# One more modulation vector computed in columns, more weight pairs multiplied by seven products, and deeper buffers of the weights' parts

## The chip, the cores and the metric

The kernel runs on one core of one Trainium2 chip. Its time is the device time of one execution in microseconds (us); lower is better. The core has a matrix engine (TensorE, PE in the profile, PEld for its weight loads), a vector engine (VectorE, DVE), an activation engine (ScalarE, ACT), a general engine (GpSimd, POOL), and SyncE (SP), which only issues DMA transfers here. Each engine works its own instructions off strictly in program order and waits on semaphores for the others.

## What is computed

One layer of a conditioned decoder on one sequence of S = 256 tokens with D = 2048 features, all in float32:

```python
mod = silu(c) @ ada_w + ada_b                      # 2048 x 12288
sh1, sc1, g1, sh2, sc2, g2 = split(mod, 6)         # m = 0 ... 5
h = rms_norm(x, norm1_g) * (1 + sc1) + sh1
u, lru_gate, q, k, v, mix = split(h @ w_in + b_in)
y_lru = rg_lru(conv4(u)) * gelu(lru_gate)          # a scan over the tokens
y_attn = sliding_window_attention(q, k, v, sinks)
merged = sig(mix_a) * (y_lru @ w_lru_out) + sig(mix_b) * (y_attn @ w_attn_out)
x = x + g1 * (merged @ w_o)
h2 = rms_norm(x, norm2_g) * (1 + sc2) + sh2
gate, up = split(h2 @ w_ffn_in, 2)                 # 2 x 5632 columns
x = x + g2 * ((silu(gate) * up) @ w_ffn_out)
out = rms_norm(x, final_g)
```

The sixth part of `mod`, g2 (m = 5), is needed only after the last matrix product.

## The kernel before

**Products.** A float32 operand is split into a high part, which ScalarE makes by a cast to fp32r (L325), and a low part, which VectorE makes by subtracting the high part (L337). Each product of two operands is three matmuls: high by high, high by low, low by high (`mm3`, L377 to L379).

**The list of items.** All weights are read as a list of 632 items, as a rule a 128x1024 piece each. `step(i)` (L347 to L370) writes out the instructions for item i. It first issues the load of item i+5 (`AHEAD`), the high part up to item i+3 (`N_HI` = 4 buffers), the low part up to item i+2 (`N_LO` = 3 buffers), and then the item's matmuls. The cast of item i+3 takes the buffer of item i-1, so it starts on ScalarE only when TensorE is done with item i-1, and whatever stands behind it in ScalarE's queue waits with it. The same holds on VectorE for the low part of item i+2.

**Work at the side.** Between the items stands all other work: generators that give one piece of work at a time. `hmod` makes the modulated activations h of the first projection, 16 tiles (kt = 0 to 15), each by a scaling on ScalarE (`hx`, L560), a cast on ScalarE (L586) and a low part on VectorE (L565). `mixers` makes the scan and the attention. `ada` computes parts of `mod` in columns: for each 128 outputs two custom reductions on VectorE over a 128x1024 half (`aw`, L527, with the row `crow` of silu(c)). `ada_ffn` (`ada_rows`, L698 to L728) computes g2 as a row: 32 multiply-adds on VectorE into `pa` (L718), then four fp32 matmuls `pb` with a matrix of ones (L724). `run_sides` lets a generator go on when a planner's clock says that its engine has time before the end of the item. Where a product needs an h that isn't there, `hact(kt)` (L541) lets the generators go on at once, so that what is missing is written out right there. `finish` does the same for g2 at the start of slab pair 1 of the feed-forward part (`all_modulations`).

**Stages.** On TensorE the first projection (tiles `wi`) stands at 33 to 355 us, the gate columns `wgl` to 449, the output product of the scan (`wl`) to 551, the branch gates to 650, the attention's output to 740, `w_o` to 828, then slab 0 of the feed-forward input to 877.6, slab pairs 1 to 10 of 42.4 us each to 1304.8, and two sweeps over the feed-forward output (tiles `pf`) to 1529.

**Seven products.** In the feed-forward part some pairs of items are multiplied by a scheme with seven block products in place of eight (`seven()`): 21 matmuls of 512 columns for 24. It needs sums of weight blocks: `wx` by DMAs of the POOL queue with accumulation (L438, L442) and `wy` by two additions on VectorE (L453, L454), and the parts of these sums; sums of activations (`hs`, `al`) come with it. Three of eight pairs in slab pairs 1 to 10 are multiplied so, and eight of 18 in each sweep (`TURNS`).

Of the kernel before, what the change touches and what calls it, by code (L numbers as in the profile page):

```python
# [9 lines left out]
F32 = mybir.dt.float32  # L10
F32R = mybir.dt.float32r
AF = mybir.ActivationFunctionType
ALU = mybir.AluOpType
# [27 lines left out]
ADA_T = (0, 1, 2, 3, 4)  # L41

AHEAD, N_HI, N_LO, N_ADA, N_B4 = 6, 4, 3, 2, 25

N_H = 8
# [35 lines left out]
def hybrid_layer(  # L81
    ctx: ExitStack, tc, vecs, x_t, x_r, ada_k, ada_t, ada_g, w_in, bv_row, bm_row, lru_w, w_lru, w_att, w_o,
# [8 lines left out]
    ap_ = ctx.enter_context(tc.tile_pool(name="ap", bufs=1))  # L91
# [76 lines left out]
    crow = ap_.tile([P, D], F32, tag="pal", name="crow")  # L168
    c_ps = []
    for i in range(4):  # L170
        cs = slice(i * 512, (i + 1) * 512)
        nc.vector.tensor_tensor(
            crow[:, cs].rearrange("p (j n) -> p j n", n=P), ident.unsqueeze(1).broadcast_to([P, 4, P]),
            cact[:, 4 * i:4 * i + 4].unsqueeze(2).broadcast_to([P, 4, P]), op=ALU.mult,
        )
        c_ps.append(mtile(f"c_ps{i}"))
        nc.tensor.matmul(c_ps[i], lhsT=ones, rhs=crow[:, cs], start=True, stop=True)
# [337 lines left out]
    def ada_cols(todo, halves):  # L515

        yield 0, 0
        for group in todo:
            for j in range(2):
                for m, kt in group:  # L520
                    v = V_ADA + m * NK + kt
                    dst = modc[:, m, kt:kt + 1]
                    if not halves.got:
                        halves.fetch()
                    yield CH * T_DVE + 0.1, 0, 0, 0, halves.here
                    r = halves.take()
                    nc.vector.tensor_tensor_reduce(  # L527
                        out=r, in0=r, in1=crow[:, j * CH:(j + 1) * CH], op0=ALU.mult, op1=ALU.add, scale=1.0,
                        scalar=dst if j else vec[:, v:v + 1], accum_out=dst,
                    )  # L530
# [165 lines left out]
    bcs = {}  # L696

    def ada_rows():  # L698

        got = Halves([ada_g[kt, :, j * CH:(j + 1) * CH] for kt in range(NK) for j in range(2)])  # L700
        got.spare = lambda: len(got.got) - got.own < N_SPARE
        yield 0, 0, 0, 0, lambda: ada.cost is None
        streams.append(got)
        got.fetch()

        pa = ap_.tile([P, D], F32, tag="pal", name="pa")
        for h in range(2):
            yield 0, 1.9
            for kt in range(h * NK // 2, (h + 1) * NK // 2):
                v = V_ADA + 5 * NK + kt  # L710
                nc.scalar.activation(pa[:, rows(kt)], ident, AF.Copy, scale=vec[:, v:v + 1])
        for kt in range(NK):
            for j in range(2):
                if not got.got:
                    got.fetch()
                yield CH * T_DVE, 0, 0, 0, got.here
                p = pa[:, j * CH:(j + 1) * CH]
                nc.vector.scalar_tensor_tensor(p, got.take(), cact[:, kt:kt + 1], p, op0=ALU.mult, op1=ALU.add)  # L718
                got.fetch()
        for c in range(4):  # L720
            yield 0, 0, 0, 1
            pb = mtile(f"pb{c}")
            cs = slice(c * 512, (c + 1) * 512)
            nc.tensor.matmul(pb, lhsT=ones, rhs=pa[:, cs], start=True, stop=True)  # L724
            yield 0, 0.55
            nc.scalar.copy(pa[:, cs], pb)
            free(m=1)
        bcs[5] = pa  # L728
# [309 lines left out]
    g1d = dp.tile([NK, P], F32, name="g1d")  # L1038

    def gate_rows():  # L1040
        while not {(2, kt) for kt in range(NK)} <= cols_done:
            ada.advance(True)
        ps = mtile("g1_ps")
        nc.tensor.transpose(ps[0:NK, 0:P], modc[:, 2, :], ident)
        row = sp.tile([P, S], F32, tag="t2", name="g1_row")
        nc.scalar.copy(row[0:NK, 0:P], ps[0:NK, 0:P])
        free(m=1)
        nc.gpsimd.dma_start(g1d, row[0:NK, 0:P])
        for i in range(2):
            g1.append(b4(f"g1{i}", F32, (CH,)))  # L1050
            nc.gpsimd.dma_start(
                g1[i], g1d[8 * i:8 * i + 8, :].rearrange("k p -> (k p)").partition_broadcast(P)
            )

    for s in range(4):
        add_slab(w_att[s], f"wa{s}", aact, 0, NK, att_post(s), True, gate_rows if s == 3 else None)
# [7 lines left out]
    def load_rows(s):  # L1064
        def before():
            xr.append(b4(f"xr{s}", F32, (2, 512)))
            nc.sync.dma_start(xr[s], x_r[:, s * 512:(s + 1) * 512].rearrange("(t p) n -> p t n", p=P))
            if s == 3:
                ada.finish(halves.fetch)
        return before  # L1070
# [56 lines left out]
    def second_norm(banks):  # L1127
        sides[:] = [ada_ffn]
# [141 lines left out]
    def add_pair(s):  # L1270
# [55 lines left out]
        for k in range(0, NK, 2):  # L1326
            loads = [w_f1[s + 11 * n][:, k * 512:(k + 2) * 512] for n in range(2)]
            if k in SEVEN_1:
                last = k == SEVEN_1[-1]
                seven(  # L1330
                    loads, lambda j, n, k=k: w_f1[s + 11 * n][:, (k + j) * 512:(k + j + 1) * 512], False, act(k), bank,
                    k == SEVEN_1[0], last, shared if last else None,
                )
                continue
            for n in range(2):
                items.append(Item(loads[n], CH, plain(k, n), gated_rows if (k, n) == (NK - 2, 1) else None))
# [18 lines left out]
    def last_first():  # L1355
        ada_ffn.finish(streams[-1].fetch)
        fin["ss"] = const.tile([P, 2, 5], F32, name="ss3")

    def x2_of(t, a, b):
        return fin["x2", t, a // CH][:, a % CH:(b - 1) % CH + 1]  # L1360

# [9 lines left out]
    def fetch(h, *what):  # L1371

        def stage():
            cs = slice(h * CH, (h + 1) * CH)
            for t in what:
                if t == "fg":
                    x = fin["fg", h] = bp.tile([P, CH], F32, tag="b4", name=f"fg{h}")
                    nc.sync.dma_start(x, fg_row[cs].partition_broadcast(P))
                else:
# [54 lines left out]
    def combined(n):  # L1434
# [29 lines left out]
    def add_block(t, ps, c0, cols, dst=None):  # L1464
# [3 lines left out]
        nc.vector.tensor_tensor(y, ps, bcs[5][:, c0:c0 + cols], op=ALU.mult)  # L1468
# [32 lines left out]
    for n, src in ((0, w_f2a), (2, w_f2d)):  # L1501
# [95 lines left out]
    ada_ffn = Side(ada_rows())  # L1597
# [92 lines left out]
    sides.extend((hmod, ada, ada_ffn))  # L1690
# [8 lines left out]
def _layout(i):  # L1699
# [10 lines left out]
    def pairs(w):  # L1710
# [17 lines left out]
        "ada_t": a_t, "ada_g": ada_w[:, 5 * D:].reshape(NK, P, D),  # L1728
# [27 lines left out]
```

## Time and profile before

| | us |
|---|---|
| median of 3 runs (lowest, highest) | 1545.44 (1544.53, 1545.70) |
| the profiled execution | 1545.76 |
| its span, first to last instruction | 1544.0 |
| TensorE busy | 1527.5 (99%) |
| VectorE busy | 1342.4 (87%) |
| ScalarE busy | 857.5 (56%) |

The span is 1.8 us shorter than the time of the same execution; the difference lies around the first and the last instruction. The busy time of a matmul in a list of groups counts its whole way through the array (389 ns for 512 columns), while the next starts 227 ns later; costs of matmuls are therefore taken from starts.

### The profile page before, as it was taken

To read this page: it belongs to the slowest core of one execution; us is meant where nothing else is said; L and a number is where in the kernel's file an instruction comes from. 1 tells how busy PE (TensorE), PEld (TensorE's weight loads), DVE (VectorE), ACT (ScalarE), POOL (GpSimd) and SP (SyncE) were. 2 spreads that over 40 slices of the span, in tenths; PEclk is the share of its full clock that TensorE was granted. 3 is DMA by queue.
4 is the path that set the end of the run, shared out by engine and by line. 5 is a ranking of instruction groups with operands and counts; after the bars stand their busy time and mean duration, and the time that the engine had idled before them with its cause. 6 is when DMAs were issued, how large, how long until landed. Compare 5 with 4: busy or idle time off the path is not lost.

```text
span 1544.0 us, 22331 instructions
## 1 busy us (share of the span) xinstructions
PE 1527.5 (99%) x8013; PEld 1313.4 (85%) x8013; DVE 1342.4 (87%) x1762; ACT 857.5 (56%) x1113; POOL 137.5 (9%) x195
## 2 busy tenths in 40 slices
PE   8999999999999999999999999999999999999997
PEld 7999999998888787888888788888888888888886
DVE  7889989899998887988988888888888888888987
ACT  4654443776865445434545655555555556664664
POOL 0000000000000000000001231111112112211200
PEclk9999999999999999999999999999999999999999
DMA  9999998666887897999999998797788779989873
GB/s 367 371 330 333 337 320 285 228 195 200 305 283 237 287 316 266 362 340 339 368 383 357 308 289 254 218 268 227 226 245 249 234 233 283 269 250 303 269 252 123
DMA packets 133951, 436.58 MB, mean 283 GB/s; under 512 B 15424, under 2 KB 15568, under 8 KB 133840
## 3 DMA queue, kind: packets, MB, share of 16 engines
q1 hardware_dynamic: 112624, 385.33, 71.4%
q0 software_dynamic: 20928, 49.30, 13.9%
q8 instruction: 62, 1.02, 0.3%
q10 hardware_dynamic: 288, 0.52, 0.1%
q14 instruction: 49, 0.40, 0.1%
HBM read 430.90 MB, written 4.20 MB: 282 GB/s over the span
## 4 chain that ended last, share of the span: by engine, by line
PE 94%; DMA 4%; DVE 1%; ACT 0%; SPq 0%; issue 0%; DVEq 0%; ACTq 0%
PE pf L1398 10%; PE f L378 7%; PE f L379 7%; PE f L377 7%; PE wi L379 6%; PE wi L378 6%; PE wi L377 6%; PE wl L379 2%; PE wl L377 2%; PE wga L379 2%; PE wga L377 2%; PE wl L378 2%; PE wgl L377 2%; PE wgl L379 2%; PE wga L378 2%; PE wa L377 2%
## 5 line engine op out<-in xcount | busy, mean ns | idle before, releaser
L325 ACT CAST hi<-raw 128x1024 fp32r<-128x1024 f32 (+1 forms) x540 | 536.7, 1002 | 442.4 <-PE wi L378 117.4
L337 DVE TENSOR_TENSOR lo<-raw,hi 128x1024 fp32r<-128x1024 f32 (+1 forms) x540 | 616.4, 1160 | 89.6 <-issue 49.9
L379 PE MATMUL wi<-h,lo 128*128 128x256 f32 x800 | 226.8, 284 | 3.7 <-DVE lo L337 3.7
L377 PE MATMUL wi<-h,hi 128*128 128x256 f32 x800 | 227.5, 284 | 0.0
L378 PE MATMUL wi<-h,hi 128*128 128x256 f32 x800 | 226.5, 283 | 0.0
L377 PE MATMUL f<-hi,h 128*128 128x512 f32 x460 | 180.3, 392 | 0.0
L379 PE MATMUL f<-hi,h 128*128 128x512 f32 x460 | 179.1, 389 | 0.0
L378 PE MATMUL f<-lo,h 128*128 128x512 f32 x460 | 179.1, 389 | 0.0
L379 PEld LDWEIGHTS wi<-h,lo 128*128 128x128 f32 x800 | 153.6, 192 | 4.3 <-DVE lo L337 4.1
L377 PEld LDWEIGHTS wi<-h,hi 128*128 128x128 f32 x800 | 153.6, 192 | 0.4 <-ACT hi L325 0.2
L378 PEld LDWEIGHTS wi<-h,hi 128*128 128x128 f32 x800 | 153.6, 192 | 0.2
L337 DVE TENSOR_TENSOR lo<-wx,hi 128x1024 fp32r<-128x1024 f32 x46 | 56.4, 1225 | 59.1 <-PE f L378 40.2
L379 PEld LDWEIGHTS f<-hi,h 128*128 128x128 f32 x460 | 86.4, 188 | 17.9
L377 PEld LDWEIGHTS f<-hi,h 128*128 128x128 f32 x460 | 86.4, 188 | 17.8 <-issue 0.2
L378 PEld LDWEIGHTS f<-lo,h 128*128 128x128 f32 x460 | 86.4, 188 | 17.8 <-issue 0.2
L527 DVE CUSTOM_DVE_ANT_0 aw<-aw,crow,vec 128x1024 f32<-128x1024 f32 x79 | 100.6, 1278 | 0.9 <-DMA aw<-in_ada_t_dram 0.9
L527 DVE CUSTOM_DVE_ANT_0 aw<-aw,crow,modc 128x1024 f32<-128x1024 f32 x79 | 100.8, 1280 | 0.0
L325 ACT CAST hi<-wx 128x1024 fp32r<-128x1024 f32 x46 | 48.5, 1055 | 87.3 <-PE f L379 41.7
L325 ACT CAST hi<-wy 128x1024 fp32r<-128x1024 f32 x46 | 48.5, 1055 | 77.5 <-PE f L379 50.9
L1398 PE MATMUL pf<-hi,fc 128*128 128x512 f32 x256 | 71.0, 389 | 0.0
L442 POOL DMA_DIRECT2D wx<-in_w_f_dram x60 | 53.6, 944 | 148.1 <-DMA wx<-in_w_f_dram 145.7
L438 POOL DMA_DIRECT2D wx<-in_w_f_dram x60 | 38.0, 714 | 311.8 <-DVE lo L337 132.2
(355 smaller groups left out, 3044.7 us busy)
## 6 DMA issues: line engine op xcount, KB each, us to landing
raw<-in_w_in_dram SPq DMA_DIRECT2D x164, 512.0 KB, 5.2
aw<-in_ada_t_dram SPq DMA_DIRECT2D x158, 512.0 KB, 6.5
raw<-in_w_f_dram SPq DMA_DIRECT2D x146, 512.0 KB, 5.1
wx<-in_w_f_dram POOLq DMA_DIRECT2D x120, 256.0 KB, 6.3
raw<-in_w_f2a_dram SPq DMA_DIRECT2D x36, 512.0 KB, 6.5
raw<-in_w_lru_dram SPq DMA_DIRECT2D x32, 512.0 KB, 4.5
raw<-in_w_att_dram SPq DMA_DIRECT2D x32, 512.0 KB, 6.1
raw<-in_w_o_dram SPq DMA_DIRECT2D x32, 512.0 KB, 7.8
```

Of the source, the lines that this page charges most:

```text
L325: nc.scalar.copy(hi[:, cs], live[i][0][:, cs])
L337: nc.vector.tensor_tensor(lo[:, cs], raw[:, cs], f32(hi[:, cs]), op=ALU.subtract)
L377: nc.tensor.matmul(ps, lhsT=lh, rhs=rh, start=start, stop=False, skip_group_check=True)
L378: nc.tensor.matmul(ps, lhsT=lh, rhs=rl, start=False, stop=False, skip_group_check=True)
L379: nc.tensor.matmul(ps, lhsT=ll, rhs=rh, start=False, stop=stop, skip_group_check=True)
L438: nc.gpsimd.dma_start(x[:, j * 512:(j + 1) * 512], block(0, 1))
L442: nc.gpsimd.dma_start(got["x"][:, j * 512:(j + 1) * 512], block(j, j), accum_op=ALU.add)
L527: nc.vector.tensor_tensor_reduce(out=r, in0=r, in1=crow[:, j * CH:(j + 1) * CH], op0=ALU.mult, op1=ALU.add, scale=1.0, scalar=dst if j els ...
L1398: nc.tensor.matmul(bank(t, n), lhsT=l[:, rows(t)], rhs=w[:, c0:c0 + 512], start=kt == 0 and k == 0, stop=kt == (EARLY - 2 if (t, n) == (1, ...
```

## The change

Four things are changed together.

- g2 is no longer computed as a row but by `ada` in columns, as the other five parts are: the table `ADA_T` and the list `cols` get m = 5, `ada_rows` goes with its 32 additions, its `pa` and its four `pb` matmuls. `gate_rows(5)`, at the start of slab pair 1, finishes the columns, transposes them by one matmul and writes them to DRAM; the halves of the row are loaded again before the sweeps (`fetch`, tile `g2`).
- Slab pairs 2 to 8 take four of eight pairs by seven products, pair 10 two, pairs 1 and 9 three as before; each sweep takes ten of 18.
- `N_HI` goes from 4 to 5, `N_LO` from 3 to 4, `N_MADE` from 5 to 6. The memory comes from `pa`'s pool, which goes; `crow` moves into two tiles of the common pool.
- While h2 exists, `ada`'s halves may use only their two own buffers (`not h2` in `halves.spare`).

```diff
-ADA_T = (0, 1, 2, 3, 4)
-AHEAD, N_HI, N_LO, N_ADA, N_B4 = 6, 4, 3, 2, 25
+ADA_T = (0, 1, 2, 3, 4, 5)
+AHEAD, N_HI, N_LO, N_ADA, N_B4 = 6, 5, 4, 2, 25
-N_MADE, N_HOLD = 5, 4
+N_MADE, N_HOLD = 6, 4
-SEVEN = tuple(range(6, 36, 4))
-SEVEN_1, SLAB_7 = (4, 8, 12), 1
-TURNS = "--7-7-7-7-7-7-7-7-"
+SEVEN = (6, 10, 12, 14, 18, 22, 24, 26, 30, 34)
+SEVEN_1, SLAB_7 = (4, 6, 10, 12), 1
+TURNS_1 = {1: "---7-77-", 9: "--7-7-7-", 10: "--7--7--"}
+TURNS = "--77-77-77-77-77--"
...
-    crow = ap_.tile([P, D], F32, tag="pal", name="crow")
+    crow = [bp.tile([P, CH], F32, tag="b4", name=f"crow{j}") for j in range(N_C)]
...
-        pa = ap_.tile([P, D], F32, tag="pal", name="pa")
...
-                p = pa[:, j * CH:(j + 1) * CH]
-                nc.vector.scalar_tensor_tensor(p, got.take(), cact[:, kt:kt + 1], p, op0=ALU.mult, op1=ALU.add)
...
-            nc.tensor.matmul(pb, lhsT=ones, rhs=pa[:, cs], start=True, stop=True)
-            yield 0, 0.55
-            nc.scalar.copy(pa[:, cs], pb)
...
+    def ada_to(*ms):
+        while not {(m, kt) for m in ms for kt in range(NK)} <= cols_done:
+            if not ada.advance():
+                clock["pe"] += 1
+                halves.fetch()
+
+    def gate_rows(m):
+
+        ada_to(m)
+        ps = mtile(f"g{m}_ps")
+        nc.tensor.transpose(ps[0:NK, 0:P], modc[:, m, :], ident)
+        row = sp.tile([P, S], F32, tag="t2", name=f"g{m}_row")
+        nc.scalar.copy(row[0:NK, 0:P], ps[0:NK, 0:P])
+        free(m=1)
+        nc.gpsimd.dma_start(gate_d[m], row[0:NK, 0:P])
...
-                halves.spare = lambda: len(halves.got) - halves.own < N_SPARE and (
+                halves.spare = lambda: len(halves.got) - halves.own < N_SPARE and not h2 and (
...
-        sides[:] = [ada_ffn]
+        sides[:] = [ada]
...
     def all_modulations():
-        ada_ffn.finish(streams[-1].fetch)
+        gate_rows(5)
         return 0, 0
...
-    cols += [[(m, kt), (m, kt + 1)] for m in (2, 4, 3) for kt in range(0, NK, 2)]
+    cols += [[(m, kt), (m, kt + 1)] for m in (2, 4, 3, 5) for kt in range(0, NK, 2)]
```

The longer lead of the high and low parts changes what the planner's clock says, and with it the order of the work at the side, in stages that the diff doesn't name. Three places follow, each as it stands before and now. In the rows the number behind a name's letters is that of the item or the tile (`lo24` is the low part of item 24, `hx5` the scaled tile kt = 5), and the number behind the underscore is a running one. L530 now is L527 before, L538 is L535, L568 is L565, L340 is L337, L328 is L325 and L380 to L382 are L377 to L379.

**The first projection, tile kt = 5 of h**, which item 21 is the first to use. VectorE before, from the low part of item 14 on:

```order
L337 TENSOR_TENSOR lo14_751<-raw14_662,hi14_714 128x1024
L527 ISA aw20_695,modc_164<-aw20_695,crow_111,modc_164 128x1024
L527 ISA modc_164 128x1
L337 TENSOR_TENSOR lo15_789<-raw15_689,hi15_749 128x512
L527 ISA aw21_718,modc_164<-aw21_718,crow_111,modc_164 128x1024
L527 ISA modc_164 128x1
L535 SCALAR_TENSOR_TENSOR modc_164<-modc_164,vec_77 128x1
L337 TENSOR_TENSOR lo16_825<-raw16_712,hi16_787 128x1024
L565 TENSOR_TENSOR h2_167<-hx5_853,h2_167 128x256
```

VectorE now, from the low part of item 23 on:

```order
L340 TENSOR_TENSOR lo23_998<-raw23_936,hi23_961 128x1024
L530 ISA aw19_665,modc_162<-aw19_665,crow0_108,vec_74 128x1024
L530 ISA modc_162 128x1
L530 ISA aw20_687,modc_162<-aw20_687,crow1_109,modc_162 128x1024
L530 ISA modc_162 128x1
L340 TENSOR_TENSOR lo24_1032<-raw24_959,hi24_996 128x1024
L530 ISA aw21_768,modc_162<-aw21_768,crow1_109,modc_162 128x1024
L530 ISA modc_162 128x1
L538 SCALAR_TENSOR_TENSOR modc_162<-modc_162,vec_74 128x1
L568 TENSOR_TENSOR h2_165<-hx5_1041,h2_165 128x256
```

ScalarE now, at the same place:

```order
L328 CAST hi23_961<-raw23_936 128x1024
L328 CAST hi24_996<-raw24_959 128x1024
L328 CAST hi25_1030<-raw25_994 128x1024
L563 ACTIVATE hx5_1041<-xT1_78,modc_162 128x256
L589 CAST h2_165<-hx5_1041 128x256
```

The low part of h for kt = 5 stood behind the low part of item 16; now it stands behind that of item 24, and its scaling behind the cast of item 25. These are the last ones written out ahead of item 21, which uses it.

**The output product of the scan, item 154** (`wl`), which is the first to use the scan's group 3 (`yh3`, `yl3`). VectorE before, where `yl3` is made:

```order
L337 TENSOR_TENSOR lo147_4884<-raw147_4813,hi147_4861 128x1024
L527 ISA aw87_4857,modc_164<-aw87_4857,crow_111,vec_77 128x1024
L527 ISA modc_164 128x1
L337 TENSOR_TENSOR lo148_4908<-raw148_4837,hi148_4882 128x1024
L841 TENSOR_TENSOR yl3_4899<-uc3_4071,yh3_4898 128x1024
```

VectorE now:

```order
L340 TENSOR_TENSOR lo157_5055<-raw157_5011,hi157_5032 128x1024
L804 TENSOR_TENSOR ig3_4616<-ig3_4616,uc3_4614 128x1024
L814 SCALAR_TENSOR_TENSOR acc3_522<-acc3_522,r3_4615 128x1024
L818 TENSOR_TENSOR ig3_4616<-ig3_4616,acc3_522 128x1024
L822 SCALAR_TENSOR_TENSOR uc3_4614<-a3_4857,ig3_4616 128x256 x4
L824 TENSOR_TENSOR uc3_4614<-uc3_4614,acc7_581 128x1024
L832 TENSOR_TENSOR yl3_5079<-uc3_4614,yh3_5078 128x1024
L340 TENSOR_TENSOR lo158_5098<-raw158_5030,hi158_5053 128x1024
```

ScalarE now, from the cast of item 158 on; four pairs of L809 and L810 stand ahead of the first row of the second fence, behind a table load:

```order
L328 CAST hi156_5013<-raw156_4990 128x1024
L328 CAST hi157_5032<-raw157_5011 128x1024
L328 CAST hi158_5053<-raw158_5030 128x1024
L809 ACT_TABLE_LOAD
L809 ACTIVATE a3_4857<-r3_4615,nsp_173 128x256
```

```order
L812 ACTIVATE acc3_522<-a3_4857 128x1024
L816 ACT_TABLE_LOAD
L816 ACTIVATE acc3_522<-acc3_522 128x1024
L819 ACT_TABLE_LOAD
L819 ACTIVATE acc7_581<-acc7_581 128x1024
L830 CAST yh3_5078<-uc3_4614 128x1024
```

TensorE now, where item 154 begins:

```order
L382 MATMUL wl0_0_1_4934<-hi153_4951,yl2_4767 128x512
L380 MATMUL wl0_0_0_4933<-hi154_4971,yh3_5078 128x512
L381 MATMUL wl0_0_0_4933<-lo154_4994,yh3_5078 128x512
L382 MATMUL wl0_0_0_4933<-hi154_4971,yl3_5079 128x512
L380 MATMUL wl0_0_1_4934<-hi154_4971,yh3_5078 128x512
```

`yl3` stood behind the low part of item 148. Now the second half of the scan's group 3, from `ig3` to `yl3`, stands in one piece behind the low part of item 157, and on ScalarE behind the cast of item 158, the last ones ahead of item 154.

**The start of slab pair 1.** Item 292 is its first. VectorE before:

```order
L1236 TENSOR_TENSOR sg0_8383<-fu0_0_1_8393,sg0_8383 128x512
L337 TENSOR_TENSOR lo294_8570<-raw294_8496,hi294_8546 128x1024
L337 TENSOR_TENSOR lo295_8602<-raw295_8523,hi295_8568 128x1024
L472 TENSOR_TENSOR hs12_8618<-x1T6_8292 128x128
L473 TENSOR_TENSOR hs12_8618<-x1T6_8292 128x128
```

VectorE now, the first four of seven reductions in a row (`aw183` to `aw189`; the low part of item 296 stands behind them):

```order
L1216 TENSOR_TENSOR sg0_8337<-fu0_0_1_8347,sg0_8337 128x512
L340 TENSOR_TENSOR lo295_8535<-raw295_8483,hi295_8508 128x1024
L530 ISA aw183_8537,modc_162<-aw183_8537,crow0_108,vec_74 128x1024
L530 ISA modc_162 128x1
L530 ISA aw184_8539,modc_162<-aw184_8539,crow1_109,modc_162 128x1024
L530 ISA modc_162 128x1
L530 ISA aw185_8542,modc_162<-aw185_8542,crow1_109,modc_162 128x1024
L530 ISA modc_162 128x1
L530 ISA aw186_8545,modc_162<-aw186_8545,crow0_108,vec_74 128x1024
```

TensorE now, between the last matmul of slab 0 and the first of slab pair 1:

```order
L381 MATMUL fu0_0_1_8347<-lo291_8438,h2_7_8065 128x512
L382 MATMUL fu0_0_1_8347<-hi291_8414,h2_7_8065 128x512
L711 MATMUL g5_ps_8558<-ident_92,modc_162 16x128
L380 MATMUL f00_1_8563<-hi292_8436,h2_0_8058 128x512
L381 MATMUL f00_1_8563<-lo292_8461,h2_0_8058 128x512
```

Four `pb` matmuls stood at this place; now the transpose of the columns of g2 stands there, and it reads what the seven reductions write.

More of the change, by code (lines that the diff above doesn't have):

```diff
@@ L693, in hybrid_layer, with gate_half @@
             )
[L696 to L704, printed above, removed]
[L706 to L728 removed]
+    gate_d = {m: dp.tile([NK, P], F32, name=f"gate_d{m}") for m in (2, 5)}
+    def ada_to(*ms):
[11 more added lines that the diff above has]
+        nc.gpsimd.dma_start(gate_d[m], row[0:NK, 0:P])
+    def gate_half(m, h):
+        return gate_d[m][8 * h:8 * h + 8, :].rearrange("k p -> (k p)").partition_broadcast(P)
     nsp = const.tile([P, NK], F32, name="nsp")
@@ L1037, in hybrid_layer, with first_gate @@
     g1 = []
[L1038 to L1053, printed above, removed]
+    def first_gate():
+        gate_rows(2)
+        for h in range(2):
+            g1.append(b4(f"g1{h}", F32, (CH,)))
+            nc.gpsimd.dma_start(g1[h], gate_half(2, h))
     for s in range(4):
-        add_slab(w_att[s], f"wa{s}", aact, 0, NK, att_post(s), True, gate_rows if s == 3 else None)
+        add_slab(w_att[s], f"wa{s}", aact, 0, NK, att_post(s), True, first_gate if s == 3 else None)
     x1d = dp.tile([S, D], F32, name="x1d")
@@ L1335, in add_pair @@
             for n in range(2):
-                items.append(Item(loads[n], CH, plain(k, n), gated_rows if (k, n) == (NK - 2, 1) else None))
+                items.append(Item(loads[n], CH, plain(k, n), gated_rows if (k, n) == (others[-1], 1) else None))
         if s == SLAB_7:
```

49 lines of the change are left out of this document (28 added, 21 removed).

## The prediction

> **What bounds the kernel now.** I read the page's busy times and its chain first, then the stretches by stage.
>
> ```profile
> PE 1527.5 (99%) x8013; PEld 1313.4 (85%) x8013; DVE 1342.4 (87%) x1762; ACT 857.5 (56%) x1113; POOL 137.5 (9%) x195
> PE 94%; DMA 4%; DVE 1%; ACT 0%; SPq 0%; issue 0%; DVEq 0%; ACTq 0%
> 33.00:193.00 160.00, 156.29 (x1236) 152.85 (x1235) 143.77 (x204) 84.83 (x127) 0.00 (x0) 1.00 0.96 345
> 1304.80:1420.00 115.20, 115.20 (x514) 95.53 (x513) 98.31 (x106) 67.41 (x73) 25.04 (x34) 1.00 0.92 278
> 1420.00:1529.00 109.00, 109.00 (x484) 90.32 (x483) 100.27 (x110) 67.39 (x80) 11.68 (x16) 1.00 0.71 225
> L379 PE MATMUL wi<-h,lo 128*128 128x256 f32 x800 | 226.8, 284 | 3.7 <-DVE lo L337 3.7
> ```
>
> In the rows of stretches the columns are the stretch, its length, busy time of PE, PEld, DVE, ACT and POOL, the clock, the DMA share and GB/s. TensorE has hardly a gap: of the largest group's idle time 3.7 us stand in the whole run. So every matmul that goes is time gained, and every wait on TensorE that comes is time lost in full. VectorE is the next bound: 144 of 160 us in the first projection, and 92% of the last stretch. Work at the side fits only where it stands early enough in each queue, and the order shows that this has changed.
>
> **Products: a gain.** Now the page's matmul rows by their starts, at the end of slab 0.
>
> ```profile
> 875.74 0.39 PE L378 MATMUL fu<-lo,h 128*128 128x512 f32 x1
> 877.33 0.39 PE L379 MATMUL fu<-hi,h 128*128 128x512 f32 x1
> 877.56 3.59 PE L724 MATMUL pb<-pa,ones 128*128 128x512 f32 x8
> 880.59 0.80 PE L377 MATMUL f<-hi,h 128*128 128x512 f32 x1
> ```
>
> Seven matmuls lie between the first two starts: (877.33 - 875.74)/7 = 0.227 us. A pair by seven products saves three. Slab pairs 2 to 8 gain one such pair each, pair 10 loses one: 6 x 3 = 18; each sweep gains two: 12. Together 30 x 0.227 = **-6.8**. The `pb` matmuls go: 880.59 - 877.56 = **-3.0**.
>
> **The first projection: a loss.** In the order, tile kt = 5 of h now stands behind the low part of item 24 and the cast of item 25, and item 21 needs it. With five and four buffers these two wait for the end of item 20. So TensorE, done with item 20, must wait for the whole string that makes h. The trace of before has one such place, near 52 us:
>
> ```profile
> 50.52 1.05 ACT L325 CAST hi<-raw 128x1024 fp32r<-128x1024 f32 x1 [2.78 <-DMA raw<-in_w_in_dram]
> 51.47 0.60 ACT L560 ACTIVATE hx<-xT,modc 128x256 f32<-128x256 f32 x1
> 52.10 0.40 ACT L586 CAST h<-hx 128x256 fp32r<-128x256 f32 x1
> 52.54 0.42 DVE L565 TENSOR_TENSOR h<-hx,h 128x256 fp32r<-128x256 f32 x1 [2.43 <-ACT h L586]
> 54.15 0.39 PE L379 MATMUL wi<-h,lo 128*128 128x256 f32 x1 [2.04 <-DVE lo L337]
> 54.37 0.28 PE L377 MATMUL wi<-h,hi 128*128 128x256 f32 x1
> 54.97 0.28 PE L379 MATMUL wi<-h,lo 128*128 128x256 f32 x1
> ```
>
> Cast, scaling, cast, low part: 52.54 + 0.42 - 50.52 = 2.4 us in a string. That is the short form of the wait, where the columns of the modulation are there. In the long form they are not, as for kt = 5: the low part of item 24, a reduction, then scaling, cast and low part:
>
> ```profile
> 875.24 1.22 DVE L337 TENSOR_TENSOR lo<-raw,hi 128x1024 fp32r<-128x1024 f32 x1
> 876.38 1.28 DVE L718 SCALAR_TENSOR_TENSOR pa<-aw,cact,pa 128x1024 f32<-128x1024 f32 x1
> L527 DVE CUSTOM_DVE_ANT_0 aw<-aw,crow,modc 128x1024 f32<-128x1024 f32 x79 | 100.8, 1280 | 0.0
> ```
>
> A low part takes 876.38 - 875.24 = 1.14, a reduction 1.28 (1.2 from start to start), scaling to low part 52.96 - 51.47 = 1.5: 3.9 to 4.0 us. Two more reductions stand just ahead of the low part of item 24: with that of item 23 they are 1.14 + 2 x 1.2 = 3.5 us, against 24 matmuls of (54.97 - 54.37)/5 = 0.12 us, 2.9, for item 20, so VectorE comes up to 0.7 late and the wait is 4.7 to 4.9. In the order kt = 4, 6 and 12 have the short form and kt = 5, 7, 8 and 14 the long one; the place at 52 us (kt = 3) keeps its wait. Low bound: short 2.4 less one matmul, long 3.9: 3 x 2.3 + 4 x 3.9 = 22.5. High bound: short 2.6, long 5.4 (two reductions behind the low part): 29.4. I take 2.4 and 4.9: **+27**, nearer to the high end because reductions stand ahead at each long place. Nothing makes up for it: a later string starts from a TensorE that is late by the same amount, and nothing behind had been waiting for something else.
>
> **Item 154: a loss.** It needs `yh3`, and the string to it starts with the cast of item 158, which waits for the end of item 153. From the same work of an earlier group, whose pieces were spread:
>
> ```profile
> 412.13 1.28 ACT L818 ACT_TABLE_LOAD   x1
> 413.43 0.51 ACT L818 ACTIVATE a<-r,nsp 128x256 f32<-128x256 f32 x1
> 414.39 0.49 ACT L818 ACTIVATE a<-r,nsp 128x256 f32<-128x256 f32 x1
> 420.07 1.04 ACT L821 ACTIVATE acc<-a 128x1024 f32<-128x1024 f32 x1
> 424.32 1.06 ACT L825 ACTIVATE acc<-acc 128x1024 f32<-128x1024 f32 x1
> 441.90 1.05 ACT L839 CAST yh<-uc 128x1024 fp32r<-128x1024 f32 x1
> L823 DVE SCALAR_TENSOR_TENSOR acc<-acc,r x4: 1218/1222/1226, 297.4 to 421.1; 128x1024 f32<-128x1024 f32 x4
> L827 DVE TENSOR_TENSOR ig<-ig,acc x4: 1218/1219/1220, 307.2 to 427.0; 128x1024 f32<-128x1024 f32 x4
> L831 DVE TENSOR_TENSOR_SCAN uc<-a,ig x16: 662/666/686, 318.1 to 435.9; 128x256 f32<-128x256 f32 x16
> ```
>
> Cast of item 158 1.0; table 1.3; four pairs at 414.39 - 413.43 = 0.96, 3.8; square 1.0; on VectorE 1.2 beside the next table load, 1.3; root 1.1; product 1.2 (the gate's activation runs beside it and the scans); four scans 2.7; product 1.2, as L827; cast 1.0: 15.6. Two matmuls later `yl3` is needed, 1.2 - 0.5 = 0.7 more. Low bound 15, if starts overlap as they do on a full queue; high 17 with a hop at each of six changes of engine. I take **+16**.
>
> **Slab pair 1: a loss.** TensorE's transpose waits for seven reductions, which stand behind an addition and the low part of item 295; the addition waits for slab 0's last matmul, the low part for the buffer of item 291.
>
> ```profile
> 878.17 1.29 DVE L1236 TENSOR_TENSOR sg<-fu,sg 128x512 f32<-128x512 f32 x2
> ```
>
> 0.6 + 1.14 + 7 x 1.2 = 10.1, with the transpose and hops **+10.5** (the `pb` that stood here are already taken off). SP issues the seven halves in one run, behind the loads up to item 297; at the 1.5 us that 512 KB take at 345 GB/s they can be a little slower than the reductions: high bound 13. The load of item 298 waits behind them on SP, but it is needed only six items after the restart. Low bound 6, if half of the reductions start before slab 0's end. The copy and the write to DRAM of g2 have 400 us to spare. The 64 halves' reductions of m = 5 that replace 32 additions cost about the same each (1.2 us) and lie on VectorE where it isn't late, but for these seven.
>
> **The clock: a loss.** TensorE's first matmuls are slow, and after its last the clock falls.
>
> ```profile
> 1.06 2.93 PE L160 MATMUL warm<-ones 128*128 128x128 f32 x12 [1.06 <-DVE eps_t L152]
> 8.04 3.51 PE L160 MATMUL warm<-ones 128*128 128x128 f32 x30
> 1534.32 0.28 PE L379 MATMUL late<-hi,fl 128*128 128x256 f32 x1
> 1537.30:1540.00 2.70, 0.00 (x0) 0.00 (x0) 0.66 (x2) 0.10 (x1) 0.00 (x0) 0.50 0.61 240
> ```
>
> 12 matmuls take 2.93 us (0.244 each) at first, 30 take 3.51 (0.117) later: some 3 us at half pace, 1.5 us lost. The clock is 0.50 from 1537.3 on, 2.7 us after the last matmul's end at 1534.6. So a wait above about 2.7 us may cost 1.5 us more. The two long waits certainly pass that: 3.0. The four of 4 to 5.4 us may: 0 to 6, taken as half. Together **+6.0**, bounds 0 and 9.
>
> The Trainium skill ("TensorE: Matmul & The Clock Gate", "What's actually happening") says that the clock halves after a free-running idle window of about 3.4 us and needs as long a busy one to come back. By its figure each fall would cost an estimated 1.7 us, the six waits 10 in all, the two alone 3.4. The trace agrees with the kind of behaviour: 0.244 against 0.117 us, and 0.50 after the last matmul.
>
> **Last sweeps: a small loss.** A group of two sevens and a plain pair now asks VectorE for
>
> ```profile
> 1311.00 1.09 DVE L1416 TENSOR_TENSOR al<-fs,ah 128x896 fp32r<-128x896 f32 x1
> 1312.00 0.68 DVE L453 TENSOR_TENSOR wy<-wx,raw 128x512 f32<-128x512 f32 x1
> 1312.72 0.69 DVE L454 TENSOR_TENSOR wy<-wy,raw 128x512 f32<-128x512 f32 x1
> ```
>
> three low parts of 1.14, one half of 0.6, `wy` 0.7 + 0.65 and `al` 1.0 = 6.4 per seven, 2 x 6.4 + 2.3 = 15.1, against 66 matmuls, 15.0. By stretches: each sweep's VectorE gets 2 x 4.1 more, 106.5 of 113.8 us in the first and 108.5 of 107.6 in the second. It is at its limit, so some waits come: **+2.5**, bounds 0 and 8. In slab pairs 2 to 8 one more seven brings VectorE by the same count (3.1 to 4.1) to 39 to 40 of 41.7 us: no wait, with one buffer more. Two halves' `wx` on POOL's queue come more often there; a late one would add to the upper end.
>
> **Sum.** 1545.8 - 6.8 - 3.0 + 27 + 16 + 10.5 + 6 + 2.5 = **1598**, against the profiled execution; the median of the runs is 0.3 lower, which I leave. About 0.2%, 3 us, is what a measurement can tell from no change.
>
> **Rivals.** (a) *Only the two long strings count.* If ScalarE and VectorE come to kt = 4 to 15 earlier than the order suggests, for instance because the extra buffer lets casts run through while TensorE still has an item, the first projection costs nothing: 1545.8 - 9.8 + 16 + 10.5 + 3 = 1565.5. For it: the trace of before has room, 144 of 160 us on VectorE. Against it: a cast can't start before its buffer is free, and the order of a queue is fixed. 0.12. (b) *Faster.* Only the products and `pb` count: 1545.8 - 9.8 = 1536. The mechanism would be cover at all three places: the deeper buffers would have to hold TensorE's work for the strings. It decides as soon as the strings cost less than 6.7 us in all; the items written out ahead are at most 4 x 2.9 us, but they stand behind the string in the queue, which speaks against it. 0.03; that the waits just eat the gain: 0.02. (c) *VectorE binds from slab pair 2 on*, or `wx` sums come late: 5 to 8 us above the sum, 1604 to 1608: 0.13. (d) *Every wait of the first projection costs the clock*: 3 us above the sum, 1601; this is the page's rule for the gate carried to the four waits near 5 us: 0.15. The forecast as summed: 0.55.
>
> Chances: slower by over 0.2% 0.95, within 0.02, faster 0.03. The range takes (a) in at the low end, 1564, and (c) with the high bounds of the strings, 1614, at the other.
>
> **What would show it.** Right: TensorE idle some 2.4 or 5 us, waiting for L568's `h`, at seven places between 60 and 270 us; one gap of 16 us near 465 us of before's time, released by the cast L830; one of 10 us ahead of `g5_ps`, released by L530; clock below 1.00 behind these two. Slab pairs 2 to 8 at 41.7 us in place of 42.4. Wrong: no gaps for `h` (then rival a), slab pairs longer than before (c), or loads that come late everywhere, which nothing here speaks for.

## The result, and the profile after

The changed kernel takes 1619.51 us (median of 4 runs, 1616.97 to 1621.68) against 1545.57 us (4 runs) before: a ratio of 1.048, 95% interval 1.0466 to 1.0493. It is slower by 74 us; 52 were forecast, and the time lies above the range, which ended at 1614. The profiled execution took 1617.44 us with a span of 1615.7, so 71.7 us are to be found between the two profiles.

The page of the changed kernel, busy times and chain:

```profile
PE 1541.1 (95%) x7976; PEld 1320.1 (82%) x7976; DVE 1376.0 (85%) x1849; ACT 875.1 (54%) x1125; POOL 164.8 (10%) x236
PE 87%; DMA 5%; DVE 4%; ACT 2%; issue 1%; SPq 0%; DVEq 0%; ACTq 0%
```

TensorE is 95% busy where it was 99%, and the chain that ended last now runs through VectorE, ScalarE and transfers for 11% of the span, where it was 5%. What TensorE waited for stands in its waits (what was waited for, us in total, times, the longest):

```profile
PE wi L380 <- ACT h L589: 28.1, 8, 5.4
PE wl L380 <- ACT yh L830: 15.8, 1, 15.8
PE g_ps L711 <- DVE modc L530: 11.2, 1, 11.2
PE pp L382 <- DVE al L1405: 2.3, 3, 0.8
PE pf L1387 <- DVE lo L340: 2.0, 1, 2.0
PE wi L382 <- DVE lo L340: 1.9, 2, 1.4
PE r_ps L1135 <- ACT yo L1132: 1.6, 1, 1.6
```

The first three are the three places of the prediction. Most of the rest of the loss is pace. Stretches of the changed kernel, cut where the granted clock is half; the column behind POOL is the clock:

```profile
57.50:64.40 6.90, 4.02 (x18) 3.85 (x18) 1.65 (x2) 3.54 (x6) 0.00 (x0) 0.51 0.99 390
84.80:88.25 3.45, 3.45 (x19) 3.45 (x18) 1.23 (x1) 2.18 (x5) 0.00 (x0) 0.51 0.39 140
...
511.50:528.60 17.10, 5.92 (x13) 4.23 (x14) 7.79 (x9) 8.27 (x11) 0.00 (x0) 0.50 0.00 0
945.00:955.20 10.20, 4.30 (x11) 3.43 (x12) 5.85 (x10) 1.06 (x3) 3.31 (x5) 0.50 0.58 220
sum 58.15, PE 36.99 PEld 33.92 DVE 22.00 ACT 18.56 POOL 3.84; mean PE 4.11 PEld 3.77 DVE 2.44 ACT 2.06 POOL 0.43
```

There are nine such stretches, 58 us together. TensorE works in 37.0 us of them, at half pace, so 18.5 us are lost. The kernel before has none between its first 5 us and its last matmul: its clock is 1.00 in every stage from 33 to 1529 us.

### The profile page after: what moved, and what is told of

The parts are those of the page before. It is cut to its first block, busy times and chain, and to the rows that moved or that the text cites. A ratio compares the mean times of both kernels' runs of the same rounds, so it can differ in the third digit from the quotient of the medians.

```text
span 1615.7 us, 22386 instructions
## 1 busy us (share of the span) xinstructions
PE 1541.1 (95%) x7976; PEld 1320.1 (82%) x7976; DVE 1376.0 (85%) x1849; ACT 875.1 (54%) x1125; POOL 164.8 (10%) x236
## 3 DMA queue, kind: packets, MB, share of 16 engines
q0 software_dynamic: 25440, 59.80, 15.8%
## 4 chain that ended last, share of the span: by engine, by line
PE 87%; DMA 5%; DVE 4%; ACT 2%; issue 1%; SPq 0%; DVEq 0%; ACTq 0%
PE pf L1387 7%; PE wi L381 6%; PE f L380 6%; PE f L381 6%; PE f L382 6%; PE wi L380 6%; PE wi L382 6%; PE wl L380 2%; PE wl L382 2%; PE wl L381 2%; PE wga L382 2%; PE wga L380 2%; PE wga L381 2%; PE wa L382 2%; PE wgl L380 2%; PE wgl L382 2%
## 5 line engine op out<-in xcount | busy, mean ns | idle before, releaser
L328 ACT CAST hi<-raw 128x1024 fp32r<-128x1024 f32 (+1 forms) x540 | 532.7, 994 | 568.9 <-PE wi L381 150.5
L340 DVE TENSOR_TENSOR lo<-raw,hi 128x1024 fp32r<-128x1024 f32 (+1 forms) x540 | 612.5, 1148 | 135.8 <-issue 58.5
L380 PE MATMUL wi<-h,hi 128*128 128x256 f32 x800 | 233.7, 292 | 28.1 <-ACT h L589 28.1
L382 PE MATMUL wi<-h,lo 128*128 128x256 f32 x800 | 231.5, 289 | 1.9 <-DVE lo L340 1.9
L381 PE MATMUL wi<-h,hi 128*128 128x256 f32 x800 | 232.6, 291 | 0.4
L380 PEld LDWEIGHTS wi<-h,hi 128*128 128x128 f32 x800 | 159.0, 199 | 30.0 <-ACT h L589 29.7
L380 PE MATMUL f<-hi,h 128*128 128x512 f32 x424 | 166.9, 394 | 0.0
L382 PE MATMUL f<-hi,h 128*128 128x512 f32 x424 | 165.8, 391 | 0.0
L381 PE MATMUL f<-lo,h 128*128 128x512 f32 x424 | 165.7, 391 | 0.0
L381 PEld LDWEIGHTS wi<-h,hi 128*128 128x128 f32 x800 | 159.1, 199 | 2.1 <-DVE h L568 1.9
L382 PEld LDWEIGHTS wi<-h,lo 128*128 128x128 f32 x800 | 158.9, 199 | 2.3 <-DVE lo L340 2.3
L530 DVE CUSTOM_DVE_ANT_0 aw<-aw,crow,vec 128x1024 f32<-128x1024 f32 x95 | 120.8, 1278 | 0.1
L530 DVE CUSTOM_DVE_ANT_0 aw<-aw,crow,modc 128x1024 f32<-128x1024 f32 x95 | 120.8, 1278 | 0.0
L382 PEld LDWEIGHTS f<-hi,h 128*128 128x128 f32 x424 | 80.0, 189 | 16.9
L380 PEld LDWEIGHTS f<-hi,h 128*128 128x128 f32 x424 | 80.1, 189 | 16.3
L328 ACT CAST hi<-wy 128x1024 fp32r<-128x1024 f32 x56 | 59.0, 1054 | 56.6 <-PE f L382 29.2
L340 DVE TENSOR_TENSOR lo<-wy,hi 128x1024 fp32r<-128x1024 f32 x56 | 68.3, 1220 | 17.1 <-PE f L381 16.7
L340 DVE TENSOR_TENSOR lo<-wx,hi 128x1024 fp32r<-128x1024 f32 x56 | 68.3, 1219 | 10.0 <-issue 7.5
L445 POOL DMA_DIRECT2D wx<-in_w_f_dram x72 | 64.5, 984 | 80.1 <-DMA wx<-in_w_f_dram 79.0
L441 POOL DMA_DIRECT2D wx<-in_w_f_dram x72 | 42.5, 693 | 288.6 <-DVE lo L340 117.8
L328 ACT CAST hi<-wx 128x1024 fp32r<-128x1024 f32 x56 | 58.9, 1052 | 16.2 <-PE f L382 13.3
```

Source lines behind the costliest of these rows:

```text
L328: nc.scalar.copy(hi[:, cs], live[i][0][:, cs])
L340: nc.vector.tensor_tensor(lo[:, cs], raw[:, cs], f32(hi[:, cs]), op=ALU.subtract)
L380: nc.tensor.matmul(ps, lhsT=lh, rhs=rh, start=start, stop=False, skip_group_check=True)
L381: nc.tensor.matmul(ps, lhsT=lh, rhs=rl, start=False, stop=False, skip_group_check=True)
L382: nc.tensor.matmul(ps, lhsT=ll, rhs=rh, start=False, stop=stop, skip_group_check=True)
L441: nc.gpsimd.dma_start(x[:, j * 512:(j + 1) * 512], block(0, 1))
```

## The experiments

The question was where 72 us come from: three strings of work that the deeper buffers put late (theory A), g2's columns (B), the extra sevens (C), and how much of it is clock.

**e1, the buffers of before in the changed kernel.**

```diff
-AHEAD, N_HI, N_LO, N_ADA, N_B4 = 6, 5, 4, 2, 25
+AHEAD, N_HI, N_LO, N_ADA, N_B4 = 6, 4, 3, 2, 25
-N_MADE, N_HOLD = 6, 4
+N_MADE, N_HOLD = 5, 4
```

> The changed kernel with four, three and five (N_HI, N_LO, N_MADE) as before; columns and sevens stay. Theory A (all long waits come from the order that the deeper buffers bring about): the waits for h, for yh at item 154 and for the seven reductions at slab pair 1 are gone, the clock stays full; 1545.8 - 6.8 - 3.0 and 0 to 6 us of waits in the last sweeps: 1536 to 1542. Theory B (the extra reductions of g2 and the loads of its halves hold VectorE or the queues up): the waits stay in good part, above 1575. Theory C (the extra sevens bind): slab pairs 2 to 8 near 42.4 us and sweeps longer than before, above 1545.

Measured: 1561.91 us, ratio 1.0107 (1.0092 to 1.0122). Its waits:

```profile
PE pf L381 <- DVE lo L340: 8.5, 10, 0.9
PE pf L1387 <- DVE lo L340: 5.2, 1, 5.2
PE wi L382 <- DVE lo L340: 3.5, 2, 1.8
PE g_ps L711 <- DVE modc L530: 3.1, 1, 3.1
```

The waits for h and yh are gone, and that for the reductions shrinks to 3.1 us; the first projection is as long as before. So theory A holds for the three places, and g2's columns do not cause them, but for these 3.1 us. What makes them was not separated: the columns themselves, or the fourth change (`not h2` in `halves.spare`), which no run takes back. The time is 20 us above what was expected: ten times in the sweeps TensorE waits for a low part, 0.9 us at most, and once 5.2 us. The ten waits are gone in e3, with four low parts: with three, ten of 18 pairs by seven products are more than VectorE can deliver in time, and the deeper buffers are there for a reason. The wait of 5.2 us has another cause: just ahead of it VectorE stands still for 7.5 us, until g2 has been read back (see e6).

**e2, TensorE kept busy in the ten waits.**

```diff
+WARM = {8: 21, 15: 7, 21: 16, 26: 7, 32: 18, 38: 16, 60: 6, 73: 18, 154: 64, 292: 45}
...
+        if i in WARM:
+            keep_warm(WARM[i])
         for stage in it.before:
             charge(*stage())
```

> The changed kernel with matmuls on a matrix of ones put ahead of the ten waits (items 8, 15, 21, 26, 32, 38, 60, 73, 154, 292), somewhat shorter than each wait, so that TensorE is busy while it would wait. The waits' ends are set by VectorE and ScalarE and stay where they are. Clock theory (each wait costs whole stretches of half clock behind it): pace behind the waits is full, about 19 us less than the changed kernel, 1597 to 1602. Rival (the clock's cost is small, as the prediction had it, and the rest of the miss is elsewhere): 6 us less at most, above 1610.

Measured: 1605.24 us, 14.3 less than the changed kernel (9.6 between the two profiled executions), with a mean clock of 0.994 (0.980 without that edit). The same two stretches of time as above:

```profile
57.50:64.40 6.90, 6.90 (x59) 6.77 (x58) 2.23 (x3) 4.40 (x9) 0.00 (x0) 1.00 0.99 387
511.50:528.60 17.10, 16.20 (x63) 12.93 (x64) 7.97 (x8) 4.92 (x6) 0.00 (x0) 0.90 0.46 143
```

The added matmuls compute nothing that is used, VectorE, ScalarE and GpSimd work through the same order as without them, and the waits' ends stay: item 154's first matmul starts 16.2 us behind the last one of item 153 in both runs (506.50 to 522.65 us, here 495.70 to 511.87). So 14 us come back by nothing but the clock. The 19 us expected were too many: in the profiled execution four pieces of 3.4 us at half clock remain, each close to a wait of 1.5 to 2.1 us that is left. One lies at item 154, whose matmuls fill the second row here (0.90).

**e3, deep buffers and more slack for the planner.**

```diff
-SLACK = (2.0, 2.0)
+SLACK = (4.5, 3.5)
```

> The changed kernel with the deeper buffers, but the planner's slack, by which work at the side may run past the end of an item, 4.5 and 3.5 us in place of 2.0 and 2.0. In its order h, yh and the reductions stand items ahead of their use again. Theory A: deep buffers cost nothing as such, the late place of the side work does: 1536 to 1541. Rival D (the deeper buffers themselves cost: casts nearer to the loads, so that every late load stops ScalarE): above 1550 with waits for raw in the first projection.

Measured: 1547.36 us, ratio 1.0013 (1.0004 to 1.0023). All three kinds of long wait are gone with the buffers deep, so it is the order, not the depth, that costs. Its waits, which cover the 6 us above the expectation:

```profile
PE pt L1096 <- DVE xr L1117: 2.9, 2, 1.9
PE pf L1387 <- DVE lo L340: 2.4, 1, 2.4
PE wi L382 <- DVE lo L340: 2.1, 1, 2.1
PE pp L382 <- DVE al L1405: 1.7, 2, 0.8
PE r_ps L1135 <- ACT yo L1132: 1.4, 1, 1.4
```

**e4, the changed kernel with the sevens of before** (three of eight, eight of 18).

```diff
-SEVEN = (6, 10, 12, 14, 18, 22, 24, 26, 30, 34)
+SEVEN = tuple(range(6, 36, 4))
-SEVEN_1, SLAB_7 = (4, 6, 10, 12), 1
-TURNS_1 = {1: "---7-77-", 9: "--7-7-7-", 10: "--7--7--"}
+SEVEN_1, SLAB_7 = (4, 8, 12), 1
+TURNS_1 = {}
-TURNS = "--77-77-77-77-77--"
+TURNS = "--7-7-7-7-7-7-7-7-"
...
-        turns = TURNS_1.get(s, "--77-77-")
+        turns = TURNS_1.get(s, "--7-7-7-")
```

> The changed kernel with the sevens of before (three of eight, eight of 18). Theory A: the long waits stay; products 6.8 us more, nine reductions in a row at slab pair 1 in place of seven (2.4 more), 5 us of waits in the sweeps gone: 1616 to 1624. Theory C (the sevens bind): under 1605.

Measured: 1621.96 us in one run. The long waits are all there (28.1, 15.8 and 12.8 us); theory C falls.

**e5, loads one item earlier, slack as it was.** The memory for it is one common buffer (24 for 25).

```diff
-AHEAD, N_HI, N_LO, N_ADA, N_B4 = 6, 5, 4, 2, 25
+AHEAD, N_HI, N_LO, N_ADA, N_B4 = 7, 5, 4, 2, 24
```

> The changed kernel with weights loaded one item earlier (AHEAD 7, one common buffer less); hi, lo and made buffers stay deep, slack stays 2.0. Theory P (the planner holds ScalarE and VectorE for busy until the data of the next cast land; the deeper high parts left one item between load and cast where there were two, so no side work seemed to fit): the order is near that of before again, the three kinds of wait are gone: 1541 to 1549, as e3. Rival (the depth of high and low parts alone sends the side work late, whatever the loads do): above 1590.

Measured: 1544.94 us, ratio 1.0002 (0.9993 to 1.0011). One wait of size is left, 4.3 us at slab pair 1 (`g_ps`), and 1.6 us in a sweep. So the distance between load and use decides: the planner's clock sets an engine to the time when the data of the piece just written out land. That this is the way was read in the code; the run shows that loading earlier moves the order (table below).

**e10 and e11, which of the two buffers.** The changed kernel with five high and three low parts, and with four and four (and `N_MADE` 5).

```diff
-AHEAD, N_HI, N_LO, N_ADA, N_B4 = 6, 5, 4, 2, 25
+AHEAD, N_HI, N_LO, N_ADA, N_B4 = 6, 5, 3, 2, 25
```

> The changed kernel with five buffers of high parts and three of low parts. If the depth of the low parts is what sends the side work late (the planner holds VectorE for busy until the cast of the fourth item ahead, which was loaded only two items before): no long waits but one of 2 us, and the sweeps short of low parts as in e1: 1555 to 1566. If the depth of the high parts does it: 1590 or more.

```diff
-AHEAD, N_HI, N_LO, N_ADA, N_B4 = 6, 5, 4, 2, 25
+AHEAD, N_HI, N_LO, N_ADA, N_B4 = 6, 4, 4, 2, 25
-N_MADE, N_HOLD = 6, 4
+N_MADE, N_HOLD = 5, 4
```

> The changed kernel with four buffers of high parts and four of low parts. If the depth of the low parts does it: still later side work than in the changed kernel, longer waits for h (50 to 57 us in the first projection in place of 28), 28 reductions in a row ahead of slab pair 1 (about 34 us more wait there), item 154 as before the change: 1640 to 1690. If the depth of the high parts does it: as e1, 1560.

Measured: 1585.46 and 1691.78 us, one run each. The waits of e10, five high and three low:

```profile
PE wl L380 <- ACT yh L830: 15.8, 1, 15.8
PE pf L1387 <- DVE lo L340: 5.9, 1, 5.9
PE wi L380 <- ACT h L589: 5.4, 1, 5.4
PE pf L381 <- DVE lo L340: 4.0, 10, 0.4
```

and of e11, four and four:

```profile
PE wi L380 <- ACT h L589: 46.3, 10, 7.3
PE g_ps L711 <- DVE modc L530: 37.7, 1, 37.7
PE pp L382 <- DVE al L1405: 6.9, 10, 1.2
...
PE wl L382 <- DVE yl L832: 3.1, 1, 3.1
```

Neither expectation was right as it stood. The depth of the low parts makes h and the reductions late (46.3 and 37.7 us in e11, 5.4 and nothing of note in e10); the whole string of item 154 comes with the five high parts (15.8 us in e10, 3.1 in e11). e10's expectation had overlooked that string. What e5's expectation says of the high parts is thus true for item 154 only.

The order can be counted in the traces, low part by low part on VectorE:

| stands behind low part | before | changed | e1 | e3 | e5 | e10 | e11 |
|---|---|---|---|---|---|---|---|
| low part of h, kt = 5 (used by item 21) | 16 | 24 | 16 | 16 | 18 | 18 | 24 |
| `yl3` (used by item 154) | 148 | 157 | 148 | 149 | 153 | 156 | 157 |

Where the number is 24, TensorE waits for this tile; where it is 16 or 18, it does not.

**e6, e3 with g2 fetched earlier.** The reads of g2 are new in the changed kernel. VectorE there, in the first sweep (start, duration, in brackets the idle time before and what ended it):

```profile
1456.89 1.23 DVE L340 TENSOR_TENSOR lo<-raw,hi 128x1024 fp32r<-128x1024 f32 x1 [0.43 <-ACT hi L328]
1463.70 0.69 DVE L1432 TENSOR_TENSOR yv<-v,g 128x512 f32<-128x512 f32 x1 [5.58 <-DMA g<-gate_d]
1466.33 0.69 DVE L1433 TENSOR_TENSOR x<-yv,x 128x512 f32<-128x512 f32 x1 [1.94 <-DMA x<-x1d]
```

It stands still 5.6 us for g2 and 1.9 us for the residual that was fetched behind it. The read was issued at 1454.7 us, 9.0 us ahead of its use. In e4, with the sweeps of before, its use comes 11.1 us behind its issue, and neither VectorE nor TensorE waits.

```diff
-            items[end - 12].before.append(fetch(0, "g2", 0, 1))
+            items[end - 18].before.append(fetch(0, "g2", 0, 1))
```

> e3 with the first halves of g2 and of the residual fetched six items earlier in the first sweep. Theory G (the reload of g2, which the changed kernel adds, lands late and holds VectorE 6 us and TensorE 2.5 us): that wait is gone, 2.5 to 4 us less than e3: 1543 to 1545. Rival (VectorE has too much to do in the sweeps with ten of 18, and the wait only moves): 1547, as e3.

Measured: 1543.40 us, ratio 0.9990 (0.9981 to 0.9999). The wait (2.4 us on TensorE in e3) is gone, and the time is 4 us less than e3's: theory G. The rest of the 4 us was not traced.

**e7 and e8, mixes.** e7 is e1 with eight of 18 in the sweeps (`SEVEN` and `TURNS` of before), e6's fetch, and

```diff
-        if s == SLAB_7:
+        if s == 6:
             items[start].before.append(all_modulations)
```

e8 is e6 with this last edit.

> e1 (buffers of before, g2 in columns, four of eight in slab pairs 2 to 8) with the sweeps' eight of 18 of before, the transposed g2 at slab pair 6 in place of 1, and the first halves of g2 fetched six items earlier. Theory A with S (the 17 us that e1 lost against before in the sweeps come from ten of 18 with only three low parts): sweeps 224 us again, no wait at slab pair 1: 1545 - 3.0 - 4.1 and 0 to 3 us for slab pairs that took 42.0 in e1 in place of 41.7: 1537 to 1541. Rival (the sweeps lose by the late g2 alone): 1545 or more, as the ten of 18 would have been a gain.

> e6 with the transposed g2 at slab pair 6 in place of 1. Theory A: no wait at the start of slab pair 1 beyond 1 us: 1541 to 1545. Rival (the wait in the second norm and slab pair 1 of e3, 5 us, has nothing to do with g2's columns): as e6.

Measured: e7 1540.77 us (0.9970, 0.9957 to 0.9982), e8 1541.20 us (0.9976, 0.9966 to 0.9985). Both are faster than before. In e7's list the longest entry on TensorE is two waits of 3.7 us together early in the first projection, which the kernel before has too; the others, of 1.1 us or less, are those of before. In e8 1.9 and 1.0 us of the second norm stay, with 1.8 us for `al`.

**e9 and e12, e5 mended.** e9 is e5 with the transposed g2 at slab pair 6 and e6's fetch; e12 is e9 with eight of 18 in the sweeps.

> e5 (loads one item earlier, slack 2.0) with the transposed g2 at slab pair 6 in place of 1 and the first halves of g2 fetched six items earlier. e5 still waits 4.5 us with 2.2 us of slow pace behind it at slab pair 1 and 1.8 us in the first sweep; both should go: 1536 to 1539, the fastest so far. Rival (the waits move on, as in e8): 1541.

> e9 with the sweeps' eight of 18 of before in place of ten. In e9 the sweeps take 224.6 us, with three waits for the low parts of activations of 0.6 to 1 us; 12 matmuls fewer should have made them 221.2. If VectorE's limit eats the gain of ten of 18: the sweeps stay at 224 us and the time within 1 us of e9, 1536 to 1538. If the ten of 18 pay with these loads: 12 matmuls more, 1539 to 1540.

Measured: e9 1537.12 us (0.9947, 0.9934 to 0.9961), e12 1536.28 us (0.9944, 0.9930 to 0.9958). Both are faster than the kernel before by more than 8 us (0.5%); between the two the runs show no difference. Rows of e9, its sweeps and the first of its waits:

```profile
1295.60:1408.00 112.40, 112.24 (x498) 92.02 (x497) 101.72 (x111) 70.52 (x78) 28.81 (x40) 1.00 0.95 295
1408.00:1520.20 112.20, 110.60 (x485) 90.44 (x484) 108.22 (x122) 71.80 (x86) 17.34 (x24) 1.00 0.74 232
```

```profile
PE pp L382 <- DVE al L1405: 1.8, 3, 0.8
```

In the second sweep VectorE is busy for 108.2 of 112.2 us, and the activations' low parts `al` come late three times. e12 has 12 matmuls more and no such wait. So ten of 18 in the sweeps pay nothing, even where all else is in place.

## Why the prediction was wrong

Direction and places were right, and so were the three strings. The sum was short, by 19 us between the profiled executions. Point by point, measured on the waits and rows above:

| term | predicted | measured |
|---|---|---|
| matmuls and `pb` saved | -9.8 | not seen apart; slab pairs as forecast, below |
| first projection | +27 | 28.1 + 1.9 - 3.7 before = +26.3 |
| item 154 | +16 | +15.8 |
| slab pair 1 | +10.5 | +11.2 |
| the clock | +6 | +18.5 |
| last sweeps, waits | +2.5 | 2.3 + 2.0 = +4.3 |
| second norm | nothing | +1.6 |

With -9.8 the right column makes 67.9 of the 71.7 us. The cause of the other 4 us was not traced. By the first starts of the stages' tiles, 1.9 lie in the first projection (41.6 us longer, of which waits are 26.3 and clock 13.4) and 1.9 in the sweeps (3.5 longer, where waits of 4.3 less 2.7 for matmuls saved make 1.6). A part may lie in the starts just behind each wait, such as 83.99 to 84.45 in the rows below.

**The step that failed is the clock's size.** The prediction said "The four of 4 to 5.4 us may: 0 to 6, taken as half" and bounded the term by 9. The runs show 18.5: five waits of 4.0 to 5.4 us in the first projection lose 10.0, where four were taken at 3.0; two short waits there lose 3.4, where nothing was taken; the two long ones lose 5.1, where 3.0 were taken. Three things were thus wrong. First, waits of 2 us can do it too. TensorE at item 15, at the first short wait:

```profile
81.75 0.28 PE L382 MATMUL wi<-h,lo 128*128 128x256 f32 x1
83.99 0.38 PE L380 MATMUL wi<-h,hi 128*128 128x256 f32 x1 [1.96 <-ACT h L589]
84.45 0.39 PE L381 MATMUL wi<-h,hi 128*128 128x256 f32 x1
84.67 0.28 PE L382 MATMUL wi<-h,lo 128*128 128x256 f32 x1
84.79 0.37 PE L380 MATMUL wi<-h,hi 128*128 128x256 f32 x1
84.95 0.42 PE L381 MATMUL wi<-h,hi 128*128 128x256 f32 x1
85.17 0.42 PE L382 MATMUL wi<-h,lo 128*128 128x256 f32 x1
```

The wait ends at 83.99; TensorE comes to full pace (84.67 to 84.79, 0.12 us), and only at 84.8, behind the wait, does the pace halve (84.95 to 85.17, 0.22) for one stretch of 3.4 us. The 2.7 us that the prediction took as a threshold, read from the one fall at the end, were none. Second, long waits cost more than one such piece: 10.2 us of half clock at slab pair 1 and 17.1 at item 154, of which TensorE works 4.3 and 5.9. Third, all seven waits above 4 us had their stretch, two of the five in the first projection one of two pieces, while the forecast had two for certain and four by halves. e2 gives 14 us back by keeping TensorE busy, which shows the cause and not only the sum. The 1.5 us per fall were near enough: 3.45 us at half pace are 1.7 lost. The prediction's estimate by the Trainium skill's figure, 1.7 per fall, is met where TensorE works through one whole piece; its count of six waits was not: there were nine stretches, and the longest has five pieces.

**First projection.** The string is as it was predicted for the long form; ScalarE and VectorE at item 38 (kt = 8). TensorE's last matmul ahead of that wait starts at 161.74, the next one at 166.05:

```profile
161.58 1.05 ACT L328 CAST hi<-raw 128x1024 fp32r<-128x1024 f32 x1 [1.82 <-PE wi L381]
164.97 0.60 ACT L563 ACTIVATE hx<-xT,modc 128x256 f32<-128x256 f32 x1 [2.33 <-DVE modc L538]
165.60 0.40 ACT L589 CAST h<-hx 128x256 fp32r<-128x256 f32 x1
```

```profile
161.23 1.28 DVE L530 CUSTOM_DVE_ANT_0 aw<-aw,crow,modc 128x1024 f32<-128x1024 f32 x1
...
162.44 1.22 DVE L340 TENSOR_TENSOR lo<-raw,hi 128x1024 fp32r<-128x1024 f32 x1
163.57 1.28 DVE L530 CUSTOM_DVE_ANT_0 aw<-aw,crow,modc 128x1024 f32<-128x1024 f32 x1
```

The reductions ahead make VectorE 0.7 late, then come low part, reduction, scaling, cast. Two errors cancel in the +27: the single waits are shorter than taken (4.2 us here for 4.9: TensorE goes on with the cast h, at 166.0, before its low part is there), and the place at 52 us did not "keep its wait" of 2.0: it became the longest, 5.4 us. That 27 came so near to 26.3 is in part luck.

**Last sweeps.** VectorE's limit was right (`al`, 2.3 us), but 2.0 us have another cause that the prediction left out: it gave the copy and the write of g2 to DRAM "400 us to spare". That holds for the write; the read back is fetched just ahead of its use, and e6 shows what it costs. **Rivals.** (a) and (b) fall with the waits themselves. (c) falls too: slab pairs 2 to 8 kept the forecast pace (below). (d) had the right mechanism, with 3 us where 12 were due.

**Slab pairs** are as forecast: the transposes `ft` of pairs 5 to 8 of the changed kernel start from 1126.9 to 1252.8, those of four pairs before from 1056.0 to 1183.8, so three steps take 125.9 us in place of 127.8, 0.6 less each where 0.68 was worked out.

## What to carry to other kernels

Where a planner decides the order by a modelled clock, a buffer's depth is an input to the order: read the order anew at each place where work stands last ahead of its use. Where TensorE is the bound, add to each wait of 4 us or more at least one whole stretch of 3.4 us at half pace (all seven had one here), reckon with one behind some of the shorter ones (two of the six between 1.4 and 2.0 us), and count the falls, not only the waits. A value that goes through DRAM has a read as well as a write: ask when the read is issued.

## What the runs showed of the hardware that was not expected

The half-clock stretches come in whole pieces of 3.41 us: 3.45, 6.9, 10.2 and 17.1 us in the rows above are one, two, three and five of them. Their starts lie whole pieces apart too: from 57.5 to 84.8 us are eight, from there to 105.3 six, and to 142.9 eleven. Whether a wait of about 2 us brings one does not depend on its length alone. Waits of 1.7 and 2.0 us in the kernel before were followed by none. In the changed kernel a wait of 1.96 us that ended at 83.99 us was followed by one, and one of the same 1.96 us that ended at 122.94 by none:

```profile
122.94 0.38 PE L380 MATMUL wi<-h,hi 128*128 128x256 f32 x1 [1.96 <-ACT h L589]
119.00:136.00 17.00, 14.97 (x123) 14.57 (x122) 12.17 (x17) 7.18 (x8) 0.00 (x0) 1.00 0.79 255
```

e4 has the same wait of 1.60 us near 230 us as the changed kernel, yet the clock fell behind it in the changed kernel (first row) and not in e4 (second):

```profile
226.00:240.00 14.00, 12.33 (x88) 11.92 (x87) 9.55 (x15) 4.08 (x6) 0.00 (x0) 0.88 0.86 298
226.00:240.00 14.00, 12.32 (x100) 11.92 (x100) 11.06 (x15) 5.38 (x7) 0.00 (x0) 1.00 0.93 321
```

A free-running window would explain both, in which it matters how a wait lies across its edges; the Trainium skill ("TensorE: Matmul & The Clock Gate", "What's actually happening") tells of such a window of 3413 ns. The length agrees; that a fall needs an idle window does not, since the stretch from 81.4 to 84.8 ahead of the fall was only some 60% idle. It would also give a kernel with many waits a time that differs between runs: the four runs of the changed kernel have spans of 1615.2, 1615.7, 1619.8 and 1619.9 us at mean clocks of 0.982, 0.980, 0.977 and 0.976.
